# First layer's modulation in eight channel blocks, fed into two projections that grow together, with the softplus moved behind them

## The chip, the cores and the metric

The kernel runs on one core of one Trainium2 chip. TensorE (PE in the profile) does the matmuls and transposes, VectorE (DVE), ScalarE (ACT) and GpSimd (POOL) do elementwise work, and DMA queues started from SyncE (SP), ACT or POOL move data between HBM and on-chip memory. A time is the device time of one launch in microseconds (us). Three runs of the kernel before gave 1446.84, 1443.05 and 1445.64 us; their median is 1445.64 us.

## The reference, cut to what matters

Two layers of a backbone over 256 context tokens and 1024 latent tokens, 1024 channels wide. Each layer first makes a shift and a scale out of a conditioning vector and modulates its input with them:

```python
def adaln(cond, w, b):
    return jnp.split(jax.nn.silu(cond) @ w + b, 3, axis=-1)
...
shift, scale, gate = adaln(c, ada_w[layer], ada_b[layer])
shift_c, scale_c, gate_c = adaln(c_ctx, ada_w[layer], ada_b[layer])
u_lat = h_lat * (1.0 + scale[:, None, :]) + shift[:, None, :]
u_ctx = h_ctx * (1.0 + scale_c) + shift_c
```

The first layer projects u with one 1024 x 3072 matrix. Eight of the 24 column blocks go through a short convolution into a gated linear recurrence run in both directions, four into a Fourier mix, and twelve are SiLU gates. The recurrence needs, for each channel and direction, the constant softplus(-lambda):

```python
r = jax.nn.sigmoid(g[0])
i = jax.nn.sigmoid(g[1])
log_a = -LRU_C * r * jax.nn.softplus(-lam.astype(jnp.float32))
a = jnp.exp(log_a)
b = jnp.sqrt(-jnp.expm1(2.0 * log_a)) * (i * xc.astype(jnp.float32))
```

The second layer is latent attention. Nothing in it is changed.

## The kernel before, in words

Channels lie on partitions, so that u is eight tiles of 128 channels by 1280 tokens (kt = 0 to 7). Every fp32 operand of a projection is split in a high part (`uh`, `w0h`) and a low part (`ul`, `w0l`), and a product is three matmuls: high x high, high x low, low x high. A projection of one column block (`in0`, tile `z`) is eight steps kt of nine matmuls: three operand pairs by token pieces of 512, 512 and 256. PSUM holds two such `z` tiles and two small tiles of 512 columns (`gtile`); a third `z` can begin when whoever reads the first one is done with it.

The order of the work is set by a scheduler of the tile framework, which places the instructions of each engine by estimated times; each engine then runs its own list strictly in order. At the start of the kernel the program gives, in the order of the string `ORD`:

- the softplus constants `vpos` and `vneg` (L105 to L132), some thirty tiny DVE operations and one Exp on ACT;
- the conditioning vector, through SiLU, as `cond` (L146 to L152);
- the modulation in four parts of 256 channels (`ada_part`, L211): eight 256 KB tiles of weights, 32 small matmuls (two instructions each), a copy out of PSUM (`adarow`, L221), a transpose (`adatr`, L223), and additions into `mod` (L227, L230);
- `u0(kt)` (L234): load of the x tile, DVE multiplies and adds in place (`xt`, L241), ACT casts to `uh`, DVE subtracts to `ul` (the helper `split`, L80 to L82).

Then come `silu_gate(0)`, which projects block 12 and multiplies it with its own sigmoid (`sg`, L300 and L301), and `conv(0)`, which projects block 0 and convolves it (`xc`, L313 to L317). Both projections are issued beside the modulation; the entries of `IA` hold back two of their steps until given parts of the modulation are done. `conv(1)` projects block 1 (`z1` here), with the gates of head block 0 (`gps`) spread between its steps. The second layer's modulation weights (`adam`, L166, L179) are used up in eight steps beside these.

All loads of this stretch are issued by SP, in one list, with at most eight in flight.

Of the kernel before, what the change touches and what calls it, by code (L numbers as in the profile page):

```python
# [54 lines left out]
def _body(ctx, tc, ap, out, dbg=None):  # L55
# [49 lines left out]

    lam = vv("lam", 0, 16)
    vpos = const.tile([P, 16], F32, name="vpos")
    vneg = const.tile([P, 16], F32, name="vneg")  # L110
# [7 lines left out]
    V.tensor_scalar(out=t2, in0=t1, scalar1=2.0, scalar2=None, op0=ALU.add)
    V.reciprocal(out=t2, in_=t2)
    V.tensor_tensor(out=t1, in0=t1, in1=t2, op=ALU.mult)  # L120
    V.tensor_tensor(out=t2, in0=t1, in1=t1, op=ALU.mult)
    NS = 8
    V.tensor_scalar(out=vneg, in0=t2, scalar1=2.0 / (2 * NS + 1), scalar2=2.0 / (2 * NS - 1), op0=ALU.mult, op1=ALU.add)
    for k in range(NS - 2, -1, -1):
        V.tensor_tensor(out=vneg, in0=vneg, in1=t2, op=ALU.mult)
        V.tensor_scalar(out=vneg, in0=vneg, scalar1=2.0 / (2 * k + 1), scalar2=None, op0=ALU.add)
    V.tensor_tensor(out=vneg, in0=vneg, in1=t1, op=ALU.mult)
    V.tensor_scalar(out=t0, in0=t0, scalar1=0.0, scalar2=None, op0=ALU.max)
    V.tensor_tensor(out=vpos, in0=vneg, in1=t0, op=ALU.add)
    V.tensor_scalar(out=vneg, in0=vpos, scalar1=-8.0, scalar2=None, op0=ALU.mult)  # L130
    V.tensor_scalar(out=vpos, in0=vpos, scalar1=8.0, scalar2=None, op0=ALU.mult)
    sp_c()  # L132
# [74 lines left out]
    a0_p, a0_c = pool("adaw0", 8, side="right")  # L207

    ada_end = {}

    def ada_part(h):  # L211
        acc = gtile(f"ada0{h}")
        for kt in range(KT):
            w = a0_p.tile([P, 512], F32, tag="adaw", name=f"adaw0{h}{kt}")
            load(w, ap["ada_0"][h, kt])
            for j in range(4):
                mm = TE.matmul(acc[32 * j : 32 * j + 32, 0:P], cond[:, kt, :], w[:, P * j : P * j + P],
                               start=(kt == 0), stop=(kt == KT - 1), tile_position=(0, 32 * j))
            ada_end[h, kt] = mm.ins
        row = a0_p.tile([P, P], F32, tag="row", bufs=2, name=f"adarow0{h}")  # L220
        V.tensor_copy(out=row, in_=acc[:, 0:P])  # L221
        tr = gtile(f"adatr0{h}")
        TE.transpose(tr[:, 0:P], row, ident)  # L223

        bias = vv("adab0", 0, 16).rearrange("p (s h i) -> p s h i", s=2, i=2)
        for m in range(2):
            V.tensor_tensor(out=mod[:, 0, m, :].rearrange("p (s h i) -> p s h i", s=2, i=2)[:, :, h, :],  # L227
                            in0=tr[:, 0:P].rearrange("p (s i r) -> p s i r", s=2, r=32)[:, :, :, m],
                            in1=bias[:, :, h, :], op=ALU.add)
        V.tensor_scalar(out=mod[:, 0, :, 8 + 2 * h : 10 + 2 * h], in0=mod[:, 0, :, 8 + 2 * h : 10 + 2 * h],  # L230
                        scalar1=1.0, scalar2=None, op0=ALU.add)

    xt_p, xt_c = pool("xt", 3, side="right")

    def u0(kt):
        x = xt_p.tile([P, T], F32, tag="xt", name=f"xt{kt}")
        load(x, ap["x_cm"][:, kt, :])
        cuts = (0, NC, 512, T) if kt in CUT else (0, NC, T)
        for a, b in zip(cuts, cuts[1:]):
# [3 lines left out]
        cuts = (0, 512, T) if kt in CUT else (0, T)  # L243
        for a, b in zip(cuts, cuts[1:]):
# [14 lines left out]
    def in0(m, work=()):  # L259
        wh, wl = ws.pop(m) if m in ws else w0_load(m)  # L260
        z = z_ps.tile([P, 1536], F32, tag="z", name=f"z{m}")
        for kt in range(KT):

            with tc.issue_after(ada_end[IA[m, kt]]) if (m, kt) in IA else ExitStack():
                for wi, ui in ((wh, uh), (wh, ul), (wl, uh)):
                    for a, n in CH3:
                        TE.matmul(z[:, a : a + n], wi[:, kt, :], ui[kt][:, a : a + n],  # L267
# [1121 lines left out]
```

## Time and profile before

| | |
|---|---|
| median of three runs | 1445.64 us |
| the profiled execution's own time | 1445.85 us |
| its span in the trace | 1444.0 us |
| PE busy in the span | 1396.4 us (97%) |
| DVE, ACT, POOL busy | 911.3, 542.2, 678.7 us |
| mean granted TensorE clock | 0.992 |
| first matmul of a projection | at 16.84 us |
| first matmul of `z1` | at 63.47 us |

The span is 1.85 us shorter than the execution's time. Shares of the whole span are means over stages with very different limits; the change touches the first 65 us only, and is read there, from the timeline and from the chain of waits.

### The profile page before, as it was taken

To read this page: it belongs to the slowest core of one execution; us is meant where nothing else is said; L and a number is where in the kernel's file an instruction comes from. 1 tells how busy PE (TensorE), PEld (TensorE's weight loads), DVE (VectorE), ACT (ScalarE), POOL (GpSimd) and SP (SyncE) were. 2 spreads that over 40 slices of the span, in tenths; PEclk is the share of its full clock that TensorE was granted. 3 is DMA by queue.
4 is the path that set the end of the run, shared out by engine and by line. 5 is a ranking of instruction groups with operands and counts; after the bars stand their busy time and mean duration, and the time that the engine had idled before them with its cause. 6 is when DMAs were issued, how large, how long until landed. Compare 5 with 4: busy or idle time off the path is not lost.

```text
span 1444.0 us, 19804 instructions
## 1 busy us (share of the span) xinstructions
PE 1396.4 (97%) x7912; PEld 1019.3 (71%) x7912; DVE 911.3 (63%) x1454; ACT 542.2 (38%) x664; POOL 678.7 (47%) x314
## 2 busy tenths in 40 slices
PE   6998999999999999999999999999999999999997
PEld 3776777777888878887987765666565556554686
DVE  5659868665755443236844546658576757564798
ACT  2276666656112221103432143443434344445210
POOL 1124434444201233412232158767766876799643
PEclk9999999999999999999999999999999999999999
DMA  8713233233302474321043131111101010124432
GB/s 301 249 52 113 98 114 105 93 106 107 126 16 91 147 243 136 114 78 34 16 146 113 52 99 37 37 46 47 53 16 37 30 38 16 39 70 146 133 131 88
DMA packets 65869, 134.10 MB, mean 93 GB/s; under 512 B 5864, under 2 KB 31720, under 8 KB 63472
## 3 DMA queue, kind: packets, MB, share of 16 engines
q1 hardware_dynamic: 63328, 124.83, 27.0%
q0 software_dynamic: 2016, 7.60, 1.4%
q8 instruction: 62, 1.02, 0.3%
q10 hardware_dynamic: 432, 0.39, 0.1%
q14 instruction: 31, 0.25, 0.1%
HBM read 101.14 MB, written 24.66 MB: 87 GB/s over the span
## 4 chain that ended last, share of the span: by engine, by line
PE 74%; DVE 16%; DMA 3%; ACT 2%; issue 2%; POOL 1%; SPq 0%; DVEq 0%; POOLq 0%; ACTq 0%
PE s L1078 12%; PE z L267 11%; PE y L646 10%; PE po L1094 9%; PE mx L977 6%; PE yf L1212 5%; PE in1g L85 2%; PE in1g L87 2%; PE in1g L86 2%; DVE xc L317 2%; DVE gate L367 1%; DVE th L362 1%; DVE gate L378 1%; DVE m L979 1%; DMA woraw<-in_wo 1%
## 5 line engine op out<-in xcount | busy, mean ns | idle before, releaser
L1084 POOL TENSOR_TENSOR ra<-ra,p 128x1024 f32<-128x1024 f32 x112 | 269.8, 2409 | 99.3 <-ACT p L1080 95.3
L979 DVE TENSOR_REDUCE m<-mx 128x1 f32<-128x512 f32 (+1 forms) x384 | 209.4, 589 | 76.0 <-PE mx L977 75.1
L1080 ACT ACTIVATE p<-s 128x1024 f32<-128x1024 f32 x160 | 163.5, 1025 | 175.4 <-PE s L1078 171.9
L267 PE MATMUL z<-uh,w0h 128*128 128x512 f32 (+1 forms) x576 | 149.6, 366 | 4.4 <-ACT uh L76 4.4
L82 POOL TENSOR_TENSOR w0l<-w,w0h 128x1024 fp32r<-128x1024 f32 x24 | 64.0, 2666 | 184.7 <-DVE w0h L78 102.3
L267 PE MATMUL z<-ul,w0h 128*128 128x512 f32 (+1 forms) x576 | 147.7, 362 | 0.0
L267 PE MATMUL z<-uh,w0l 128*128 128x512 f32 (+1 forms) x576 | 147.5, 361 | 0.0
L267 PEld LDWEIGHTS z<-uh,w0h 128*128 128x128 f32 x576 | 98.2, 190 | 33.3 <-issue 11.5
L267 PEld LDWEIGHTS z<-ul,w0h 128*128 128x128 f32 x576 | 96.7, 190 | 18.7 <-issue 1.2
L267 PEld LDWEIGHTS z<-uh,w0l 128*128 128x128 f32 x576 | 96.3, 190 | 18.3 <-issue 2.0
L1078 PE MATMUL s<-R,KR 64*128 64x512 f32 (+1 forms) x640 | 104.9, 392 | 0.0
L345 ACT ACTIVATE gate<-gps,vec 128x512 f32<-128x512 f32 (+1 forms) x96 | 57.5, 616 | 103.3 <-PE gps L87 103.1
L977 PE MATMUL mx<-Kh,Qh 64*128 64x512 f32 (+1 forms) x384 | 86.4, 396 | 1.8 <-DVE m L979 1.5
L1094 PE MATMUL po<-p,v_even 128*64 128x512 f32 x320 | 77.5, 605 | 0.0
L1094 PE MATMUL po<-p,v_odd 128*64 128x512 f32 x320 | 77.5, 605 | 0.0
L977 PEld LDWEIGHTS mx<-Kh,Qh 64*128 64x128 f32 x384 | 43.0, 185 | 48.6 <-DVE m L979 26.8
L977 PE MATMUL mx<-KR,R 64*128 64x512 f32 (+1 forms) x384 | 77.1, 357 | 0.0
L381 POOL TENSOR_TENSOR gate<-gate,gate 128x1280 f32<-128x1280 f32 x8 | 23.9, 2990 | 112.3 <-DVE gate L378 97.1
L1078 PEld LDWEIGHTS s<-R,KR 64*128 64x128 f32 (+1 forms) x640 | 64.7, 184 | 12.3
L1078 PE MATMUL s<-Qh,Kh 64*128 64x512 f32 x320 | 70.6, 413 | 0.5 <-DVE sg L1024 0.5
L649 DVE TENSOR_TENSOR n<-gbc,y 128x1024 f32<-128x1024 f32 x10 | 12.2, 1222 | 87.3 <-PE y L646 87.3
L1078 PE MATMUL s<-Qh,Kl 64*128 64x512 f32 x320 | 67.3, 390 | 0.0
(358 smaller groups left out, 3091.2 us busy)
## 6 DMA issues: line engine op xcount, KB each, us to landing
w<-in_w SPq DMA_DIRECT2D x24, 512.0 KB
adaw<-in_ada SPq DMA_DIRECT2D x32, 256.0 KB
adawm<-in_ada SPq DMA_DIRECT2D x8, 1024.0 KB
adawg<-in_ada_g SPq DMA_DIRECT2D x8, 1024.0 KB
y_dr<-sg SPq DMA_DIRECT2D x10, 640.0 KB
woraw<-in_wo SPq DMA_DIRECT2D x12, 512.0 KB
xt<-in_x_cm SPq DMA_DIRECT2D x8, 640.0 KB
yra<-y_dr SPq DMA_DIRECT2D x10, 512.0 KB
```

The lines of the kernel that those rows point to most:

```text
L82: el.tensor_tensor(out=lo, in0=src, in1=f(hi), op=ALU.subtract)
L85: TE.matmul(o, lh, rh, start=start, stop=False)
L267: TE.matmul(z[:, a : a + n], wi[:, kt, :], ui[kt][:, a : a + n], start=(kt == 0 and ui is uh and wi is wh), stop=(kt == KT - 1 and wi is wl))
L345: S.activation(out=gt[d, g][:, a : a + n], in_=ps[:, :n], func=AF.Sigmoid, bias=vv("gateb", 4 * j + i))
L646: TE.matmul(ps[:, 512 * hf : 512 * hf + 512], a[k], b[k][:, 512 * hf : 512 * hf + 512], start=(k == 0 and a is yh and b is woh), stop=(k = ...
L977: TE.matmul(ps[a][:, :n], q[r, P * t : P * t + P], k[r, a0 : a0 + n], start=st, stop=not st)
L979: V.tensor_reduce(out=m3s[t][:, a, i : i + 1], in_=ps[a][:, :n], axis=AX.X, op=ALU.max)
L1078: TE.matmul(ps[:, a, :], k[r, ks], w[r, c], start=(j == 0), stop=(j == len(parts) - 1))
L1080: S.activation(out=es, in_=ps, func=AF.Exp, scale=SCALE)
L1084: G.tensor_tensor(out=ra, in0=st["e"][0] if kt == 1 else ra, in1=es, op=ALU.add)
L1094: TE.matmul(st["o"][64 * a : 64 * a + 64, :], quad[q][6][:, k, 128 * i + 64 * a : 128 * i + 64 * a + 64], st["e"][k][:, a, :], start=(k == ...
L1212: TE.matmul(ps[i], a[:, k, :], b[k][:, pieces[i]], start=(k == 0 and a is oh and b is w1o), stop=(k == 7 and a is ol))
```

## The change

- The weights of the first modulation are laid out for eight blocks of 128 channels instead of four parts of 256: four loads of 256 KB each a block (`ada_load`), 16 small matmuls (two instructions each) and a copy (`ada_block`), one transpose of 64 rows and two additions (`ada_turn`). The "1 +" of the scale is put into the bias once (`ab0`), instead of into each part of `mod`.
- Block kt of the modulation now serves exactly tile kt of u. For kt = 0 to 7 the projections 12 and 0 both take step kt, with the turn of block kt+1 in the middle of projection 12's step and the matmuls of block kt+2 behind it.
- All of this stands in `tc.manual_schedule`: PE, DVE, ACT and POOL keep the order of the program text there.
- The conditioning vector is loaded first; block 12's weights, the identity and the small vectors are loaded from ACT's queue, the rest from SP's.
- The softplus (`decay`) is called after the last step of the two projections. Its text and the scheduler's list both place it there.

```diff
+    first = ExitStack()
+    first.enter_context(tc.manual_schedule(engines={e.engine for e in (TE, V, S, G)}))
...
+    def decay():
...
+        S.activation(out=t1, in_=t1, func=AF.Exp)
+        V.tensor_scalar(out=t2, in0=t1, scalar1=2.0, scalar2=None, op0=ALU.add)
...
+        for k in range(NS - 2, -1, -1):
+            V.tensor_tensor(out=vneg, in0=vneg, in1=t2, op=ALU.mult)
+            V.tensor_scalar(out=vneg, in0=vneg, scalar1=2.0 / (2 * k + 1), scalar2=None, op0=ALU.add)
...
+    def ada_load(h):
+        a0s[h] = [a0_p.tile([P, 2, 256], F32, tag="adaw", name=f"adaw0{h}{i}") for i in range(4)]
+        for i in range(4):
+            load(a0s[h][i], ap["ada_0"][h][:, 2 * i : 2 * i + 2, :])
...
+    def ada_block(h):
+        acc = gtile(f"ada0{h}")
         for kt in range(KT):
-            w = a0_p.tile([P, 512], F32, tag="adaw", name=f"adaw0{h}{kt}")
-            load(w, ap["ada_0"][h, kt])
-            for j in range(4):
-                mm = TE.matmul(acc[32 * j : 32 * j + 32, 0:P], cond[:, kt, :], w[:, P * j : P * j + P],
-                               start=(kt == 0), stop=(kt == KT - 1), tile_position=(0, 32 * j))
+            for j in range(2):
+                TE.matmul(acc[32 * j : 32 * j + 32, 0:P], cond[:, kt, :], a0s[h][kt // 2][:, kt % 2, P * j : P * j + P],
+                          start=(kt == 0), stop=(kt == KT - 1), tile_position=(0, 32 * j))
+        a0r[h] = a0_p.tile([64, P], F32, tag="row", bufs=2, name=f"adarow0{h}")
+        V.tensor_copy(out=a0r[h], in_=acc[0:64, 0:P])
+
+    def ada_turn(h):
         tr = gtile(f"adatr0{h}")
+        TE.transpose(tr[:, 0:64], a0r[h], ident[0:64, 0:64])
...
     def in0(m, work=()):
-        wh, wl = ws.pop(m) if m in ws else w0_load(m)
+        if m in z0s:
+            for u in work:
+                u()
+            return z0s.pop(m)
+        wh, wl = w0_load(m)
...
+    ada_load(0)
+    u_load(0)
+    w = w_p.tile([P, KT, P], F32, tag="w", name="w0_12")
+    S.dma_start(out=w, in_=ap["w0"][12])
+    S.dma_start(out=ident, in_=ap["ident"])
+    S.dma_start(out=vec, in_=ap["vec"])
...
+    for m in (12, 0):
+        z0s[m] = z_ps.tile([P, 1536], F32, tag="z", name=f"z{m}")
...
+    for kt in range(1, KT):
+        if kt + 2 < KT:
+            ada_load(kt + 2)
+            u_load(kt + 2)
+        in0_part(12, kt, 0)
+        if kt + 1 < KT:
+            ada_turn(kt + 1)
+            u0(kt + 1)
+        in0_part(12, kt, 1)
+        if kt + 2 < KT:
+            ada_block(kt + 2)
+        in0_part(0, kt)
+    decay()
+    first.close()
```

`in0_part(12, kt, 0)` is the first five matmuls of a step (the three of `uh` x `w0h`, two of `ul` x `w0h`), `in0_part(12, kt, 1)` the other four.

How the list of VectorE changes where the two projections end. Before (`w0h_626` and `w0h_820` are the weights of blocks 1 and 2, `sg_522` the gate of block 12, `z_449` its projection, `ul_135` the last low part of u):

```order
L82 TENSOR_TENSOR ul_135<-xt_435,uh_127 128x1280 [waits Activation_49]
L78 CAST w0h_626<-w_1_624 128x1024 [waits DMAHW6_49,PE_49,Pool_49]
L301 TENSOR_TENSOR sg_522<-sg_522,z_449 128x1280 [waits Activation_49]
L78 CAST gh_616<-gw_614 128x512 [waits DMAHW0_49]
L78 CAST w0h_820<-w_2_818 128x1024 [waits DMAHW7_49,PE_49,Pool_49]
L179 COPY adarow_148<-adam_600 128x512 [waits PE_49]
L317 SCALAR_TENSOR_TENSOR xc_606<-z_525,vec,xc_606 128x255 [waits Activation_49]
```

And now, from the last low part of u (`ul_99`) to the first softplus steps behind block 2's weights (`w0h_848`; `w0h_654` are block 1's):

```order
L80 TENSOR_TENSOR ul_99<-xt_489,uh_91 128x1280 [waits Activation_49]
L118 TENSOR_SCALAR sp_583<-vec 128x16
L119 TENSOR_TENSOR sp_584<-vec,sp_583 128x16 [waits DVE_49]
L76 CAST w0h_654<-w_1_652 128x1024 [waits DMAHW6_49,PE_49,Pool_49]
L121 TENSOR_SCALAR sp_585<-sp_584 128x16 [waits Activation_49]
L122 RECIPROCAL sp_585<-sp_585 128x16 [waits DVE_49]
L123 TENSOR_TENSOR sp_584<-sp_584,sp_585 128x16 [waits DVE_49]
L76 CAST w0h_848<-w_2_846 128x1024 [waits DMAHW7_49,PE_49,Pool_49]
L124 TENSOR_TENSOR sp_585<-sp_584 128x16 [waits DVE_49]
```

Behind these come five more softplus steps, the copy of `adam` out of PSUM (L178) and fifteen softplus steps, of which the last stand here with what follows them (`sg_623` and `z_181` belong to block 12, `z_182` to block 0):

```order
L131 TENSOR_SCALAR sp_583<-sp_583 128x16
L132 TENSOR_TENSOR vpos<-vneg,sp_583 128x16 [waits DVE_49]
L133 TENSOR_SCALAR vneg<-vpos 128x16 [waits DVE_49]
L134 TENSOR_SCALAR vpos<-vpos 128x16 [waits DVE_49]
L355 TENSOR_TENSOR sg_623<-sg_623,z_181 128x1280 [waits Activation_49]
L371 SCALAR_TENSOR_TENSOR xc_634<-z_182,vec,xc_634 128x255 [waits Activation_49]
```

The gate of block 12 stood ahead of block 2's weights; it now stands behind them and behind the whole softplus.

How the list of TensorE changes. Before, where the second part of the modulation stands between matmuls of projection 12 (`ada_231` is the modulation, `z_449` the projection):

```order
L267 MATMUL z_449<-uh_120,w0h_209 128x256
L217 MATMUL ada_231<-adaw_232,cond 32x128 [waits DMAHW6_49,PE_49]
L217 MATMUL ada_231<-adaw_232,cond 32x128 x3
L267 MATMUL z_449<-ul_128,w0h_209 128x512 [waits DVE_49]
L217 MATMUL ada_231<-adaw_238,cond 32x128 [waits DMAHW7_49]
L217 MATMUL ada_231<-adaw_238,cond 32x128 x3
L267 MATMUL z_449<-ul_128,w0h_209 128x512 [waits DVE_49]
```

And now, in the middle of one step of the loop (`adatr_331` is the turn for the next block, `ada_343` the block after that, `z_181` projection 12):

```order
L318 MATMUL z_181<-ul_94,w0h_135 128x512 [waits DVE_49]
L318 MATMUL z_181<-ul_94,w0h_135 128x512
L227 MATMUL adatr_331<-ident,adarow_305 128x64 [waits DVE_49]
L318 MATMUL z_181<-ul_94,w0h_135 128x256
L318 MATMUL z_181<-uh_86,w0l_136 128x512 x2
L318 MATMUL z_181<-uh_86,w0l_136 128x256
L220 MATMUL ada_343<-adaw_316,cond 32x128 [waits DMAHW2_49,PE_49]
L220 MATMUL ada_343<-adaw_316,cond 32x128 x3
```

The modulation is no longer strewn between projection matmuls four at a time; the turn stands behind matmuls that need the present step's `ul`.

At the end of the stretch TensorE's list now reads (`z_182` is projection 0, `adam` a piece of the second layer's modulation, `z_658` block 1's projection):

```order
L318 MATMUL z_182<-ul_99,w0h_219 128x256
L318 MATMUL z_182<-uh_91,w0l_220 128x512 x2
L318 MATMUL z_182<-uh_91,w0l_220 128x256
L165 MATMUL adam_628<-adawm_626,cond 32x512 [waits DMAHW1_49,PE_49]
L165 MATMUL adam_628<-adawm_626,cond 32x512 x3
L273 MATMUL z_658<-uh_84,w0h_654 128x512 [waits DVE_49,PE_49]
```

`z_658` takes the PSUM place of `z_181`, and so its first matmul waits for the VectorE multiplication that reads `z_181` (`sg_623`).

## Rows read from the trace of the kernel before

**Rows 1.** The page's busy time of each engine (share of the span, instructions).
```profile
PE 1396.4 (97%) x7912; PEld 1019.3 (71%) x7912; DVE 911.3 (63%) x1454; ACT 542.2 (38%) x664; POOL 678.7 (47%) x314
```

**Rows 2.** Timeline, first modulation part: start, duration, engine, line, operation, idle before.
```profile
9.60 0.20 PEld L217 LDWEIGHTS ada<-adaw,cond 128*32 128x32 f32 x8 [0.45 <-DMA adaw<-in_ada]
...
10.95 0.20 PEld L217 LDWEIGHTS ada<-adaw,cond 128*32 128x32 f32 x8 [0.47 <-DMA adaw<-in_ada]
...
12.53 0.23 DVE L227 TENSOR_TENSOR mod<-adatr,vec 128x4 f32<-128x4 f32 x2 [0.56 <-PE adatr L223]
```

**Rows 3.** Timeline, the first u tile up to the first projection matmul.
```profile
13.33 2.34 POOL L82 TENSOR_TENSOR w0l<-w,w0h 128x1024 fp32r<-128x1024 f32 x1 [12.88 <-ACT w0h L76]
13.87 2.86 DVE L241 TENSOR_SCALAR xt<-xt,mod 128x256 f32<-128x256 f32 x3 [0.91 <-DMA xt<-in_x_cm]
...
16.84 1.81 PE L267 MATMUL z<-uh,w0h 128*128 128x512 f32 x3 [4.35 <-ACT uh L76]
```

**Rows 4.** Tile xt, 0 to 60 us: count, duration ns min/median/max.
```profile
L241 DVE TENSOR_SCALAR xt<-xt,mod x18: 401/542/1945, 13.9 to 51.3; 128x256 f32<-128x256 f32 x10, 128x1024 f32<-128x1024 f32 x6, 128x768 f32<-128x768 f32 x2
L76 ACT CAST uh<-xt x10: 619/1257/1267, 16.2 to 52.2; 128x1280 fp32r<-128x1280 f32 x6, 128x512 fp32r<-128x512 f32 x2, 128x768 fp32r<-128x768 f32 x2
```

**Rows 5.** Chain of waits, 26 to 63 us: start, time on the chain, what.
```profile
26.28 0.58 PE ada L217 x8
...
27.81 0.36 PE ada L217 x8
...
42.55 0.12 PE adatr L223
...
42.69 0.24 DVE mod L227 x2
...
42.96 0.18 DVE mod L230
...
43.16 1.15 DVE xt L241 x2
...
44.33 1.27 ACT uh L76
...
45.63 2.89 DVE ul L82 x2
...
49.11 13.44 PE z L267 x69
```

**Rows 6.** Windows: length, busy time of each engine, granted clock, DMA share, GB/s.
```profile
22.00:24.00 2.00, 2.00 (x12) 1.00 (x12) 0.00 (x0) 1.04 (x1) 0.81 (x1) 1.00 1.02 406
...
120.00:122.00 2.00, 2.00 (x7) 1.61 (x7) 2.00 (x3) 2.00 (x3) 1.46 (x1) 0.50 0.00 0
122.00:124.00 2.00, 2.00 (x10) 1.68 (x9) 2.00 (x1) 1.99 (x2) 2.00 (x2) 0.74 0.00 0
```

**Rows 7.** Timeline, the hand-over from the two projections to z1.
```profile
59.07 1.49 DVE L301 TENSOR_TENSOR sg<-sg,z 128x1280 f32<-128x1280 f32 x1 [1.11 <-ACT sg L300]
...
62.06 0.77 DVE L78 CAST w0h<-w 128x1024 fp32r<-128x1024 f32 x1 [1.16 <-issue]
...
62.48 1.06 PE L166 MATMUL adam<-adawm,cond 128*32 128x512 f32 x8
...
63.47 0.85 PE L267 MATMUL z<-uh,w0h 128*128 128x512 f32 x3
...
63.61 0.69 DVE L179 COPY adarow<-adam 128x512 f32<-128x512 f32 x1 [0.79 <-PE adam L166]
```

**Rows 8.** Groups by line, one of the softplus: busy us, mean ns, idle before.
```profile
L125 DVE TENSOR_TENSOR vneg<-vneg,sp 128x16 f32<-128x16 f32 x7 | 1.2, 174 | 0.2
```

**Rows 9.** Timeline, DVE and POOL, two stretches around 220 us.
```profile
220.41 3.43 POOL L82 TENSOR_TENSOR w0l<-w,w0h 128x1024 fp32r<-128x1024 f32 x1 [0.86 <-DVE w0h L78]
...
221.50 2.36 DVE L665 TENSOR_TENSOR f<-vec,mod 128x8 f32<-128x8 f32 x1
```

**Rows 10.** Timeline, PE after a long idle time.
```profile
117.24 0.79 PE L85 MATMUL gps<-xh,gh 128*128 128x512 f32 x1 [4.00 <-DVE adarow L181]
```

More of the change, by code (lines that the diff above doesn't have):

```diff
@@ L118, in _body @@
[L118 to L126, printed above, removed]
@@ L233, in _body, with u_load @@
-    xt_p, xt_c = pool("xt", 3, side="right")
+            V.tensor_tensor(out=mod[:, 0, m, :].rearrange("p (s k) -> p s k", s=2)[:, :, h],
+                            in0=tr[:, 0:64].rearrange("p (s r) -> p s r", r=32)[:, :, m],
+                            in1=ab0.rearrange("p (s k) -> p s k", s=2)[:, :, h], op=ALU.add)
+    xt_p, xt_c = pool("xt", 3, side="right")
+    xs0 = {}
+    def u_load(kt):
+        xs0[kt] = xt_p.tile([P, T], F32, tag="xt", name=f"xt{kt}")
+        for a, b in ((0, 512), (512, T)) if kt == 0 else ((0, T),):
+            load(xs0[kt][:, a:b], ap["x_cm"][:, kt, a:b])
@@ L235, in u0 @@
     def u0(kt):
[L236 to L239, printed above, removed]
+        x = xs0.pop(kt)
+        for a, b in ((0, NC), (NC, 512), (512, T)) if kt == 0 else ((0, NC), (NC, T)):
             m = 1 if b == NC else 0
@@ L272, in in0, with w0_load @@
         return z
[L274 to L276 removed]
+    def w0_load(m, eh=V, w=None):
+        if w is None:
+            w = w_p.tile([P, KT, P], F32, tag="w", name=f"w0_{m}")
+            load(w, ap["w0"][m])
         wh = w_p.tile([P, KT, P], F32R, tag="wh", name=f"w0h_{m}")
@@ L280, in w0_load, with in0_part @@
         return wh, wl
-    ws = {}
-    for c in ORD.split():
-        i = int(c[1])
-        if c[0] == "a":
-            ada_part(i)
-        elif c[0] == "w":
-            ws[12 - 12 * i] = w0_load(12 - 12 * i, S)
-        else:
-            u0(i)
+    z0s = {}
+    ada_load(0)
[4 more added lines that the diff above has]
+    S.dma_start(out=vec, in_=ap["vec"])
+    S.activation(out=sgc, in_=cnd, func=AF.Sigmoid)
+    V.tensor_tensor(out=cond[:, :, 0:2], in0=cnd, in1=sgc, op=ALU.mult)
+    ab0 = const.tile([P, 16], F32, name="ab0")
+    V.tensor_copy(out=ab0[:, 0:8], in_=vv("adab0", 0, 8))
+    V.tensor_scalar(out=ab0[:, 8:16], in0=vv("adab0", 8, 8), scalar1=1.0, scalar2=None, op0=ALU.add)
+    ws = {12: w0_load(12, S, w)}
+    ada_load(1)
+    w = w_p.tile([P, KT, P], F32, tag="w", name="w0_0")
+    load(w, ap["w0"][0])
+    u_load(1)
+    ada_block(0)
+    ada_turn(0)
+    u0(0)
+    for m in (12, 0):
+        z0s[m] = z_ps.tile([P, 1536], F32, tag="z", name=f"z{m}")
+    def in0_part(m, kt, part=None):
+        wh, wl = ws[m]
+        three = ((wh, uh), (wh, ul), (wl, uh))
+        steps = [(a, n, *o) for a, n in CH3 for o in three] if kt == 0 else [(a, n, *o) for o in three for a, n in CH3]
+        for a, n, wi, ui in steps if part is None else steps[5 * part : 5 + 4 * part]:
+            TE.matmul(z0s[m][:, a : a + n], wi[:, kt, :], ui[kt][:, a : a + n],
+                      start=(kt == 0 and ui is uh and wi is wh), stop=(kt == KT - 1 and wi is wl))
+    ada_load(2)
+    in0_part(12, 0)
+    ada_block(1)
+    ws[0] = w0_load(0, S, w)
+    u_load(2)
+    in0_part(0, 0, 0)
+    ada_turn(1)
+    u0(1)
+    in0_part(0, 0, 1)
+    ada_block(2)
+    for kt in range(1, KT):
[12 more added lines that the diff above has]
+    first.close()
     xt_c()
```

81 lines of the change are left out of this document (32 added, 49 removed).

## The prediction, made before the run

> **What bounds the kernel now.** I read the page first: TensorE is busy in 97% of the span [rows 1], so over the whole kernel only what makes TensorE start earlier, wait less or run at a higher clock can move the end. Then I read the timeline of the first 65 us, as the change touches nothing else, and the chain of waits there.
>
> The stretch has three parts. Up to 16.84 us TensorE waits for the first tile of u: the eighth 256 KB tile of modulation weights lets its matmuls begin at 10.95 us, `mod` is ready 1.81 us later [rows 2], and two multiplications on 256 columns, which take 0.40 us at best [rows 4], take until 16.2 us (the first matmul at 16.84 us [rows 3] less the cast of 0.62 us [rows 4]), because one of them lasts 1.95 us [rows 4]: GpSimd runs its weight subtraction from 13.33 to 15.67 us, and VectorE's `xt` begun at 13.87 us stands meanwhile [rows 3]. From 16.84 to 62.48 us TensorE works nearly without a gap. At first it runs at half its rate: eight modulation instructions take 0.58 us on the chain until 26.3 us and 0.36 us from 27.8 us on [rows 5]. The granted clock of the windows shows 1.00 in that time too [rows 6], so here I go by durations: the 1.2 GHz level for 10.9 us after the first projection matmul, then 2.4 GHz. The third part is the hand-over: `adam` at 62.48 us, the first matmul of `z1` at 63.47 us [rows 7]. VectorE had multiplied block 12's gate 3 us earlier, so `z1` waited for nothing.
>
> **The change part by part.** I follow the moment at which `z1` begins, since behind it the lists of all engines do the same work.
>
> *The start.* Before the first block is complete, four tiles of modulation weights, block 12's weights (as many bytes as two tiles) and the three small loads must arrive: what had arrived before when the sixth tile's matmuls began, 9.60 us [rows 2]. Plus 1.81 us, `mod` is ready at 11.4 us. x's first half is one tile more, some 0.7 us later than 9.6 us by the step between tiles, so it is no bound. Block 12's weights now come early, GpSimd's 2.34 us on them is over by then, and two multiplications of 0.40 us and a cast of 0.62 us [rows 4] give the first projection matmul at 12.9 us, 3.9 us earlier than now.
>
> The Trainium skill ("Trainium Kernel Development and Optimization", Key Constraints) says that loads started from several queues share the same DMA engines and that a second queue only saves time in issuing. The trace before has its engines at a share of 1.02 and 406 GB/s on one queue alone [rows 6], which bears that out for the steady part; by the rule the gain of the start lies in the fewer bytes.
>
> *Step 0 and the first turn.* A step's nine matmuls take 1.75 us at the full rate (69 in 13.44 us [rows 5]), 3.5 us at half: to 16.4 us. Block 1 of the modulation, four groups of eight at 0.58 us: 18.7 us. Projection 0's first five matmuls, 2560 of a step's 3840 columns, 2.3 us: turn 1 at 21.0 us. GpSimd's low part of block 0's weights is ready about then too (its bytes land near 15 us at 0.4 MB/us [rows 6], cast and subtraction follow), so it costs nothing.
>
> *The loop.* The turn of block kt+1 stands behind two matmuls that need `ul` of block kt, and `ul` of kt+1 comes out of that turn. This is a chain through four engines: turn 0.12 us, `mod` 0.24, `xt` 1.15, `uh` 1.27, `ul` 1.45 (half of 2.89) [rows 5], 0.47 for two matmuls, and seven hand-overs of 0.02 to 0.05 us: 5.0 us. The step of 0.18 us for "1 +" [rows 5] is gone. TensorE's own work in the same time is a step of each projection, 3.5 us, block and turn with 1.4 us: 4.9 us at the full rate. So the chain and TensorE need about the same, and I take 5.0 us a block. The loads need 1.7 MB a block, 4.2 us at 406 GB/s, and are hidden. At the half rate TensorE would need twice its 4.9 us; if the half rate lasts 10.9 us from the first projection matmul, as before, it ends at 23.8 us, and the second turn comes at 26.2 us. Five blocks later the seventh turn is at 51.2 us, its `ul` 4.35 us later at 55.55 us, and fifteen matmuls (2.9 us) end both projections at 58.5 us, 4.0 us earlier than now.
>
> *The hand-over.* This is what the change pays. Counted from the end E of projection 0: projection 12 now ends only 1.75 us earlier, and `z1` needs its PSUM place. The gate's multiplication that frees it stands on VectorE behind all of the softplus but two steps, behind the weights of block 2, which wait for projection 0's last use of `w0h`, and behind the copy of `adam`. Softplus steps cost 0.174 us and a gap of 0.03 us [rows 8], 0.205 us. With VectorE alone: weights of block 2 done at E+0.35, six steps to E+1.6, copy of `adam` 0.69 us [rows 7] to E+2.3, fifteen steps to E+5.4, the multiplication of 1.49 us [rows 7] to E+6.9.
>
> GpSimd comes on top. Its subtractions for blocks 1 and 2 take 2.34 us each [rows 3] and start as soon as the cast before them is done. A multiplication on 128x8 numbers took 2.36 us when it met one [rows 9], and the multiplication of the start 1.95 us [rows 4], against 0.17 us for a step alone [rows 8]. The first subtraction runs from about E-1.5 to E+0.85 and holds the third softplus product, so block 2's weights end at E+2.0; the second runs from E+2.1 to E+4.45 and holds the next step. Then five steps to E+5.5, the copy to E+6.2, fifteen steps to E+9.3, the multiplication to E+10.8. The bounds are E+6.9 (GpSimd never in the way) and E+11.6 (both subtractions in full); I take E+10.8, as the rows show waiting to the end of GpSimd's instruction.
>
> The Trainium skill ("SBUF — State Buffer", SBUF: two separate sides) says that VectorE and GpSimd share a port pair under an exclusive lock, and that an operation with two inputs in SBUF, or a copy in a fast mode, waits for GpSimd's whole instruction. By it `z1` begins at E+10.8; without it, at E+6.9.
>
> So `z1` begins at 58.5 + 10.8 = 69.3 us instead of 63.47 us: 5.8 us later. TensorE has only `adam` in that time and is idle from E+1.0 on, nearly 10 us.
>
> *The clock behind it.* After an idle time of 4.0 us TensorE resumed at 117.24 us [rows 10] and ran at a granted clock of 0.50, the 1.2 GHz level, until about 123.0 us (0.74 in the window from 122 us) [rows 6]: 5.8 us at half, 2.9 us lost. I take the same 2.9 us for `z1`. Bounds are 0 and the 5.5 us of the kernel's start (10.9 us at half). The gates in `z1` come after four steps, 9.9 us with that clock, and the convolution, cast and split that they need take some 9 us on VectorE from `z1`'s beginning, so they add nothing.
>
> *The rest.* One more ACT table load and the Exp stand beside TensorE's last two steps and end before VectorE's third softplus step. SP's list after the stretch is the same. Both cost nothing; if the Exp were late, its table load would add up to 1.3 us.
>
> The sum: 5.8 + 2.9 = 8.7 us on the profiled execution's own time of 1445.85 us, 1454.5 us. That execution lies 0.2 us from the median, so the same number stands for the median.
>
> **Rivals.**
>
> A. *The softplus stays off the path, as the change's words say.* `z1` would wait only for the sigmoid and multiplication of block 12, to E+1.1: 59.6 us, 3.9 us earlier, no idle time, 1442.0 us. For it: ACT and VectorE have free time in the loop. Against it: block 2's weights stand before 21 softplus steps in VectorE's list, and they cannot start before projection 0 has used its last `w0h`. It decides if the steps run before E+0.3.
>
> B. *GpSimd doesn't hold the small steps.* `z1` at E+6.9, 65.4 us, 3.9 us less than forecast: 1450.6 us, and 1447.7 us if the clock also stays up over the shorter idle time. For it: steps leave gaps of only 0.03 us in which GpSimd must get in. Against it: [rows 9].
>
> C. *The half rate lasts longer in the loop.* Every block at half costs TensorE 9.8 us instead of 5.0, 4.8 us more. In the first stretch modulation matmuls were mixed among those of the projection, and the clock came up only after 10.9 us; here they come in blocks of 1.0 to 2.3 us. One block more gives 1459.3 us, two 1464.1 us. Loads below 340 GB/s would look alike.
>
> **How the numbers follow.** I give the forecast 0.5, A 0.1, B 0.2, C 0.2. The forecast's own range is 1451 to 1458 us. The whole range leaves out A and the worse half of C: 1446 to 1461 us. A measurement of this kernel tells a change from none at about 0.3%, 4.3 us. Faster than 1441.3 us is only A with a still better start, 0.05. Within 0.3% lie the rest of A, half of B and little of the forecast, 0.2. Slower has the rest, 0.75.
>
> **What would show it.** In the profile after: the first projection matmul near 13 us; turns 5 us apart, with TensorE waiting for `ul` at most some tenths of a microsecond; projection 0 ending near 58.5 us; VectorE's softplus steps behind that, one or two of them lasting 2 us or more beside GpSimd; `z1` beginning near 69 us after 10 us of idle TensorE, released by the multiplication `sg`; a granted clock of 0.50 right behind. The forecast is wrong if `z1` begins before 65 us, or if projection 0 ends after 62 us.

## The result and the profile after

The changed kernel takes 1458.7 us (median of 4 runs, 1456.4 to 1461.2), the kernel before 1446.2 us: a ratio of 1.0091, 95% interval 1.0075 to 1.0108. It is slower, by 12.5 us, where 8.7 us were forecast; the time lies inside the range of 1446 to 1461 us. The profiled execution is the slowest of the four: own time 1461.15 us, span 1459.4 us, 15.4 us over the one before. TensorE's busy time has hardly changed [rows 1]; it waits longer:

```profile
PE 1398.7 (96%) x7916; PEld 1026.0 (70%) x7916; DVE 917.9 (63%) x1462; ACT 544.1 (37%) x664; POOL 680.2 (47%) x314
```

Next the chain of waits of the changed kernel from 7.6 us on (start, time on the chain, what), which answers to [rows 3, 5]:

```profile
7.60 2.80 PE ada L220 x24
...
12.20 0.63 ACT uh L74
12.82 0.04 issue
12.87 3.87 PE z L318 x9
16.74 2.94 PE ada L220 x32
...
26.38 0.20 PE adatr L227
26.58 0.89 PE z L318 x4
27.47 1.87 PE ada L220 x32
29.34 3.01 PE z L318 x14
32.35 0.20 PE adatr L227
32.55 0.89 PE z L318 x4
```

The first projection matmul comes at 12.87 us instead of 16.84 us. From 26 us on the chain holds nothing but TensorE: four matmuls, a modulation block, fourteen matmuls, a turn, and so on, 5.97 us from turn to turn up to the seventh at 56.18 us. VectorE and ScalarE stand on it only at the start, between the first and the second turn, and behind the seventh, which is the last. In this loop the modulation block takes 1.87 us for 32 instructions.

TensorE's timeline at the hand-over [rows 7] (start, duration, engine, line, operation, count, idle before):

```profile
63.89 1.07 PE L165 MATMUL adam<-adawm,cond 128*32 128x512 f32 x8
73.71 1.40 PE L273 MATMUL z<-uh,w0h 128*128 128x512 f32 x3 [8.75 <-DVE sg L355]
74.91 1.27 PE L273 MATMUL z<-ul,w0h 128*128 128x512 f32 x3
75.97 1.18 PE L273 MATMUL z<-uh,w0l 128*128 128x512 f32 x3
76.99 0.73 PE L273 MATMUL z<-uh,w0h 128*128 128x512 f32 x3
```

The two projections end at 63.89 us, 1.4 us later than before. Then TensorE is idle for 8.75 us until VectorE's gate multiplication `sg` frees the place of `z1`. Nine matmuls take 3.28 us instead of 1.75, and from 76.99 us on the rate is full. What VectorE did meanwhile, and GpSimd beside it:

```profile
61.70 0.69 DVE L76 CAST w0h<-w 128x1024 fp32r<-128x1024 f32 x1 [0.70 <-PE z L318]
...
62.80 2.15 DVE L123 TENSOR_TENSOR sp<-sp,sp 128x16 f32<-128x16 f32 x1
64.87 0.68 DVE L76 CAST w0h<-w 128x1024 fp32r<-128x1024 f32 x1
...
65.88 2.19 DVE L128 TENSOR_TENSOR vneg<-vneg,sp 128x16 f32<-128x16 f32 x1
...
72.08 1.48 DVE L355 TENSOR_TENSOR sg<-sg,z 128x1280 f32<-128x1280 f32 x1
```
```profile
62.53 2.39 POOL L80 TENSOR_TENSOR w0l<-w,w0h 128x1024 fp32r<-128x1024 f32 x1 [42.43 <-DVE sp L121]
65.69 2.35 POOL L80 TENSOR_TENSOR w0l<-w,w0h 128x1024 fp32r<-128x1024 f32 x1 [0.77 <-PE adam L165]
```

Two products on 128x16 numbers last over 2 us, each until a subtraction of GpSimd ends; the same kind of step takes 0.17 us alone. The windows behind show the clock (length, busy time of each engine, granted clock, DMA share, GB/s):

```profile
70.00:74.00 4.00, 0.29 (x1) 0.33 (x2) 3.66 (x14) 0.00 (x0) 0.00 (x0) 0.51 0.69 257
74.00:78.00 4.00, 4.00 (x14) 3.28 (x14) 4.00 (x5) 0.00 (x0) 0.00 (x0) 0.64 0.03 11
78.00:82.00 4.00, 4.00 (x22) 3.39 (x21) 3.84 (x4) 0.00 (x0) 1.81 (x1) 1.00 0.10 17
```

So `z1` begins 10.2 us later and loses 1.5 us to the half rate: 11.7 us. At the last gate product of this layer (at 362.35 us before, 373.15 us after) the shift is 10.8 us, so nothing is added between `z1` and there, and about 1 us is won back. What the profiled execution loses beyond that arises in stages that hold the same work in the same order; other runs of the same kernel are up to 4.7 us faster, and I do not assign it.

### The profile page after: what moved, and what is told of

Read it like the earlier page. It is cut to its first block, busy times and chain, and to the rows that moved or that the text cites. A ratio compares the mean times of both kernels' runs of the same rounds, so it can differ in the third digit from the quotient of the medians.

```text
span 1459.4 us, 19829 instructions
## 1 busy us (share of the span) xinstructions
PE 1398.7 (96%) x7916; PEld 1026.0 (70%) x7916; DVE 917.9 (63%) x1462; ACT 544.1 (37%) x664; POOL 680.2 (47%) x314
## 4 chain that ended last, share of the span: by engine, by line
PE 70%; DVE 19%; issue 4%; DMA 3%; ACT 3%; POOL 1%; SPq 0%; DVEq 0%; POOLq 0%; ACTq 0%
PE s L1132 12%; PE y L700 10%; PE z L273 10%; PE po L1148 9%; PE mx L1031 6%; PE in1g L83 2%; PE in1g L85 2%; PE in1g L84 2%; PE z L318 2%; DVE xc L371 2%; DVE hf L1316 2%; DVE gate L421 1%; DVE gate L432 1%; DVE m L1033 1%; PE ada L220 1%
## 5 line engine op out<-in xcount | busy, mean ns | idle before, releaser
L80 POOL TENSOR_TENSOR w0l<-w,w0h 128x1024 fp32r<-128x1024 f32 x24 | 63.9, 2663 | 189.5 <-DVE w0h L76 102.7
L273 PE MATMUL z<-uh,w0h 128*128 128x512 f32 x528 | 136.3, 366 | 8.8 <-DVE sg L355 8.8
L273 PE MATMUL z<-uh,w0l 128*128 128x512 f32 x528 | 134.1, 360 | 0.0
L273 PE MATMUL z<-ul,w0h 128*128 128x512 f32 x528 | 133.7, 360 | 0.0
L273 PEld LDWEIGHTS z<-uh,w0h 128*128 128x128 f32 x528 | 90.3, 190 | 35.0 <-issue 20.2
L273 PEld LDWEIGHTS z<-uh,w0l 128*128 128x128 f32 x528 | 88.5, 190 | 16.2 <-issue 0.8
L273 PEld LDWEIGHTS z<-ul,w0h 128*128 128x128 f32 x528 | 88.7, 190 | 15.6
L1132 PE MATMUL s<-Ql,Kh 64*128 64x512 f32 x320 | 67.1, 391 | 0.0
```

Of the source, the lines that this page charges most:

```text
L80: el.tensor_tensor(out=lo, in0=src, in1=f(hi), op=ALU.subtract)
L1132: TE.matmul(ps[:, a, :], k[r, ks], w[r, c], start=(j == 0), stop=(j == len(parts) - 1))
```

## The experiments

Times in us; E is the start of `adam`, that is the end of the first two projections. The table puts all runs together, the text tells what each was for.

| kernel | first projection matmul | E | z1 begins | time | ratio to before (95%) |
|---|---|---|---|---|---|
| before | 16.84 | 62.48 | 63.47 | 1446.2 | 1 |
| changed | 12.87 | 63.89 | 73.71 | 1458.7 | 1.0091 (1.0075 to 1.0108) |
| e1 softplus in the loop | 12.50 | 63.26 | 66.71 | 1450.5 | 1.0028 (1.0017 to 1.0039) |
| e2 softplus at the start | 18.22 | 68.93 | 72.41 | 1454.6 | 1.0060 (1.0045 to 1.0075) |
| e3 four strips | 12.70 | 60.29 | 70.12 | 1455.5 | 1.0068 (1.0053 to 1.0083) |
| e4 two sums | 12.88 | 63.26 | 73.09 | 1458.1 | 1.0084 (1.0066 to 1.0101) |
| e5 low part on VectorE | 12.79 | 63.85 | 73.14 | 1457.8 | 1.0088 (1.0072 to 1.0104) |
| e12 both low parts | 13.11 | 63.33 | 71.53 | 1455.8, one run | |
| e7 one queue | 16.01 | 66.36 | 76.20 | 1463.0, one run | |
| e8 (as e1) | 13.80 | 64.70 | 68.16 | 1449.9 | 1.0036 (1.0024 to 1.0049) |
| e10 e1, gate first | 12.99 | 64.06 | 65.23 | 1448.5 | 1.0022 (1.0011 to 1.0033) |
| e13 gate, then softplus | 13.02 | 64.08 | 65.25 | 1450.7 | 1.0030 (1.0020 to 1.0041) |
| e9 all but the gate's place | 12.14 | 58.55 | 62.02 | 1443.6 | 0.9990 (0.9981 to 1.0000) |
| e11 all | 12.34 | 54.85 | 57.63 | 1439.7 | 0.9957 (0.9944 to 0.9970) |

**e1, the softplus in the loop.** `decay()` becomes a list of steps `dk`, and a fifth of it is issued in each of five loop steps:

```
+        for u in spread(dk, 5, kt - 1) if kt <= 5 else ():
+            u()
         in0_part(0, kt)
-    decay()
```

> The changed kernel with the softplus's instructions taken apart and put five or six at a time behind the modulation copies of loop steps 1 to 5, where VectorE is idle for 1.56 us a step. Theory: block 1's projection waited 9.9 us after the first two had ended because the gate multiplication stood behind the softplus, two of whose steps GpSimd held for 2 us each. Then the first two projections still end near 63.9 us, block 1 starts at 65 to 66 us instead of 73.7, TensorE's clock stays at 1.00 there, and the time is 1448 us (10 us less than 1458.7). Rival: the weight casts of blocks 1 and 2 and GpSimd's low parts hold that multiplication by themselves: block 1 starts at 70 us or later, 1455 us.

`z1` begins 3.45 us behind E instead of 9.8 us, and the time falls by 8.2 us: the theory holds in the main, but 66.71 us is 0.7 to 1.7 us later than it said. VectorE's timeline shows what is left:

```profile
62.84 2.00 DVE L76 CAST w0h<-w 128x1024 fp32r<-128x1024 f32 x1 [1.07 <-PE z L328]
64.76 0.41 DVE L76 CAST gh<-gw 128x512 fp32r<-128x512 f32 x1
65.09 1.47 DVE L368 TENSOR_TENSOR sg<-sg,z 128x1280 f32<-128x1280 f32 x1
```

Block 2's weight cast stands ahead of the multiplication, and beside GpSimd (subtracting from 61.90 to 64.29 us) it takes 2.00 us instead of 0.69. So the rival has a share of about 2 us. In another point the theory failed: TensorE was idle for only 2.39 us, and yet its clock fell to the half rate behind that in this execution, as the window from 68 us on shows (granted clock third from the end):

```profile
68.00:70.00 2.00, 2.00 (x7) 1.69 (x6) 2.00 (x3) 0.00 (x0) 0.63 (x1) 0.50 0.86 323
```

**e8 and e10, the gate ahead of that cast.** In e8 only the end of the fixed order moved behind `sg0`; the instruction lists came out as in e1, so e8 is a second measurement of e1. In its profiled execution TensorE was idle for 2.40 us at the same place, and the granted clock stayed at 1.00. e10 writes the casts into the fixed order:

```
+    ws[1] = w0_load(1)
     sg0 = silu_gate(0, lru)
+    ws[2] = w0_load(2)
+    first.close()
```

> The kernel with the softplus in the loop, and in addition the gate multiplication of block 12 ahead of the weight casts of blocks 1 and 2 in VectorE's list (there block 1 still waited 2.4 us, as that cast of block 2 took 2.00 us beside GpSimd). Theory: sigmoid from 61.6 us, 1.24 us, multiplication 1.48 us: block 1 starts at 64.5 instead of 66.7 us, behind the modulation of the other layer and without an idle time, the clock stays up, and the time is 1447 us (3.5 us less). Rival: GpSimd's subtraction from 61.9 to 64.3 us holds the multiplication as well: 66.5 us and 1450.5 us.

> The kernel with the softplus in the loop, and block 2's weight cast written behind the gate multiplication of block 12 in the part whose order is fixed, so that it stands behind it in VectorE's list (the edit tried before left the list as it was). Theory: sigmoid 61.6 to 62.9 us, multiplication 1.48 us: block 1 starts at 64.4 instead of 66.7 us, with no idle TensorE, time 1448 us. Rival: GpSimd's subtraction for block 1 (61.9 to 64.3 us) holds the multiplication as it held the cast: block 1 at 66 us or later, 1450 us.

In e10 TensorE no longer waits: `z1` follows `adam` at 65.23 us, 0.8 us behind the theory's 64.4 because E itself is 0.8 us later there, and the time is 1448.5 us where 1448 us were said. VectorE's row of the multiplication:

```profile
63.69 1.49 DVE L367 TENSOR_TENSOR sg<-sg,z 128x1280 f32<-128x1280 f32 x1 [0.77 <-ACT sg L366]
```

GpSimd subtracted from 62.71 to 65.17 us, and this multiplication, which reads `z` from PSUM, took its usual time. The rival falls. `z1` still begins 1.8 us later than in the kernel before: that is the slower loop, to which e3 turns.

**e13, the softplus behind, but after the gate.** The changed kernel with the casts and the gate as in e10, and `decay()` behind them:

> The changed kernel with the softplus still behind the two projections, but behind the gate multiplication of block 12 in VectorE's list, mixed with the convolution that follows. Theory: what cost 10 us is the place in the list, not the softplus: block 1 starts near 65.2 us, as in the kernel with the softplus in the loop and the gate multiplication first (1448.5 us); the convolution's cast and split end some 2 us later by nine small steps and up to 4 us more where GpSimd holds a product, so that the gates inside block 1 wait 1 to 5 us: 1449.5 to 1453.5 us. Rival: the wait only changes its place, from the start of block 1 to its gates: 1457 us.

`z1` at 65.25 us as said, 1450.7 us. What the softplus still costs appears inside `z1`, in TensorE's timeline:

```profile
74.72 0.73 PE L83 MATMUL gps<-xh,gh 128*128 128x512 f32 x2 [0.76 <-DVE xh L76]
...
77.31 0.50 PE L84 MATMUL gps<-xl,gh 128*128 128x512 f32 x1 [0.69 <-DVE xl L80]
```

Two waits of 0.7 us instead of one of 8.75. The median lies 2.3 us above that of e10, the intervals of the two overlap, and the two waits make 1.45 us: so about 1.5 to 2.3 us is what the softplus itself costs here. The rest was its place in one engine's list.

**e2, the softplus at the start.** `decay()` stands behind the two bias copies.

> The changed kernel with the softplus at the program's start again, behind the two bias copies on VectorE. Theory: its 27 steps of about 0.2 us hold the first modulation copy from 10.4 to about 14.2 us, so the first projection matmul comes at 16.7 us instead of 12.9; the loop is as long as before, the hand-over to block 1 loses its 9 us, and the time is 1452 us. So putting the softplus behind cost more (9 us) than it gave at the start (4 us). Rival: the start is covered by the loads and GpSimd's hold does not matter: 1448 us.

The size was off. The first projection matmul comes 5.35 us later, not 3.8, since here too a product met GpSimd, as VectorE's timeline shows:

```profile
10.01 2.23 DVE L128 TENSOR_TENSOR vneg<-vneg,sp 128x16 f32<-128x16 f32 x1
...
15.78 0.28 DVE L223 COPY adarow<-ada 64x128 f32<-64x128 f32 x1
```

Even so the kernel is 4.1 us faster than the changed one: moving the softplus behind saved 5.35 us at the start and cost 6.3 us between E and `z1` (9.8 against 3.5 us). `z1` begins 1.3 us earlier in e2 and at the full rate, which saves another 1.5 us; the rest of the 4.1 us I do not assign.

That saving at the start is one against e2, not against the kernel before. There the softplus stood at the start too and held nothing, as VectorE's timeline of the kernel before shows:

```profile
3.60 0.18 DVE L115 TENSOR_SCALAR sp<-vec 128x16 f32<-128x16 f32 x1 [2.45 <-DMA vec<-in_vec]
...
8.94 0.18 DVE L131 TENSOR_SCALAR vpos<-vpos 128x16 f32<-128x16 f32 x1
11.67 0.29 DVE L221 COPY adarow<-ada 128x128 f32<-128x128 f32 x1 [2.56 <-PE ada L217]
```

Its input, the bias table `vec`, was there at 3.60 us, and VectorE was idle for 2.56 us between the last step and the first modulation copy. The changed kernel loads the table later (it is there at 7.89 us, in e2 at 8.07 us); the same steps, one of them held by GpSimd, end at 15.86 us in e2, and so they stand in the way.

**e5 and e12, GpSimd out of the way.** The softplus stays; low parts of weights are subtracted on VectorE, in e5 for blocks 1 and 13 (block 2, which was meant, was missed), in e12 for 1 and 2:

```
-        wh, wl = w0_load(m)
+        wh, wl = w0_load(m, el=V if m in (1, 2) else G)
```

> The changed kernel with the low parts of the weights of blocks 1 and 2 subtracted on VectorE instead of GpSimd, the softplus where it is. Theory: two softplus products took 2.15 and 2.19 us because GpSimd's subtractions held them; without these they take 0.17 us (4.0 us less), and the two subtractions cost VectorE about 1.2 us each (1.49 us for 1280 numbers). So block 1 starts 8.3 instead of 9.9 us after the first two projections end, at about 72 us, and the time is 1457 us. Rival: the long steps have another reason than GpSimd: they stay near 2 us, the subtractions come on top, block 1 starts near 76 us, 1461 us.

> The changed kernel with the low parts of the weights of blocks 1 and 2 both on VectorE (the edit before had reached block 1's, not block 2's: one of the two long softplus products, 2.31 us, had stayed beside GpSimd's remaining subtraction, and block 1 started 9.3 us after the two projections' end). Theory: no softplus product lasts over 0.3 us; the second subtraction costs VectorE 1.23 us and saves 2.1 us: block 1 starts 8.3 to 8.5 us behind the end, near 72.3 us. Rival: a long product stays although GpSimd is idle: 9.3 us or more.

In e5 `z1` begins between what the theory and the rival said, as one subtraction stayed on GpSimd: one long product was left, the one beside the one subtraction left; in e12 none. The two timelines of VectorE, e5 and then e12:

```profile
64.57 2.31 DVE L123 TENSOR_TENSOR sp<-sp,sp 128x16 f32<-128x16 f32 x1
```
```profile
63.96 1.22 DVE L80 TENSOR_TENSOR w0l<-w,w0h 128x1024 fp32r<-128x1024 f32 x1
65.10 0.17 DVE L123 TENSOR_TENSOR sp<-sp,sp 128x16 f32<-128x16 f32 x1
```

`z1` begins 9.3 and 8.2 us behind E, 9.8 in the changed kernel. e5's time is not clear of the changed kernel's, and e12 is a single run, so the argument rests on these rows. GpSimd's holds are the cause of the long steps, and with e1 the two parts of the wait are told apart.

**e3 and e4, why a modulation block takes 1.87 us.** Each block multiplies into two of TensorE's four 32-column strips; the kernel before used four. e3 sends odd contraction blocks to the other two strips and adds the halves at the turn; e4 keeps two strips, but alternates between two sums:

```
-                TE.matmul(acc[32 * j : 32 * j + 32, 0:P], ..., tile_position=(0, 32 * j))
+                c = 32 * (j + 2 * (kt % 2))
+                TE.matmul(acc[c : c + 32, 0:P], ..., tile_position=(0, c))
```

> The changed kernel with each modulation block's products spread over four 32-column strips of TensorE again (even and odd channel blocks of the contraction apart, the halves added by two more small VectorE steps at each turn). The 32 instructions of a block took 1.87 us in two strips, and 64 in four strips took 1.96 us in the kernel before. Theory: matmuls of different strips run beside each other, and two strips halve this: the block goes to about 1.0 us, the loop's period from 5.97 to about 5.1 us, the first two projections end at 58.5 instead of 63.9 us, and block 1 still waits 10 us: 1453.5 us. Rivals: what counts is that the stationary operand changes every two matmuls (it does so here too), or the chain over VectorE and ScalarE sets the period: 5.9 us and 1459 us.

> The changed kernel with two strips as it has, but each strip's products go in turn to two accumulators (even and odd contraction blocks, in two PSUM tiles), added by one more VectorE step behind the copy. If the strips set the price of a modulation block, it stays at 1.87 us, the period at 5.97 us and the time at 1459 us. Rival: successive matmuls wait for the sum that the one before them writes in the same accumulator: then the block falls to about 1.0 us as with four strips, and the time to 1453.5 us.

TensorE's timeline in e3, then in e4, then in the kernel before (64 instructions in four strips):

```profile
47.05 0.27 PE L228 MATMUL adatr<-ident,adarow 128*128 128x128 f32 x1
...
47.96 1.08 PE L221 MATMUL ada<-adaw,cond 128*32 128x128 f32 x32
...
51.83 0.73 PE L323 MATMUL z<-ul,w0h 128*128 128x512 f32 x2 [0.25 <-DVE ul L80]
52.40 0.27 PE L228 MATMUL adatr<-ident,adarow 128*128 128x128 f32 x1
```
```profile
50.68 1.94 PE L220 MATMUL ada07e<-adaw,cond 128*32 128x128 f32 x32
```
```profile
45.05 1.96 PE L217 MATMUL ada<-adaw,cond 128*32 128x128 f32 x64
```

With four strips the same 32 instructions take 1.08 us in this view, with two 1.94 us, one sum or two. So the strips set the price. The period falls to 5.35 us, not 5.1, because now the chain binds and TensorE waits 0.25 us a turn for `ul`: E is 60.29 us and not 58.5, the time 1455.5 and not 1453.5 us.

**e7, the loads on one queue.**

```
-    S.dma_start(out=w, in_=ap["w0"][12])
+    load(w, ap["w0"][12])
```

(and likewise the identity and the bias table)

> The changed kernel with the loads of block 12's weights, the identity and the bias table started by SyncE, as all others, instead of ScalarE. Theory: only the time of issuing is lost; SyncE gets to these three after six other loads, near 5.5 us, so the weights land near 8.5 instead of 4.8 us and GpSimd's subtraction moves to about 9.5 to 12 us, where it meets VectorE's bias copies and the first multiplications: first projection matmul 0.5 to 1.5 us later than 12.9 us, all behind it as before. Rival: the second queue brought a higher load rate: then the modulation weights too land later, and the first projection matmul comes 3 us later or more.

This is a single run. The delay is 3.1 us, as the rival had it, but not for its reason: the first modulation weights came earlier than in the changed kernel (first matmuls on them at 4.64 instead of 6.48 us). Block 12's weights, issued at 4.02 us, were there only at 11.37 us (4.81 us on ScalarE's queue), and the bias table at 11.78 instead of 7.89 us, behind the loads ahead of them. ScalarE's row, VectorE's and TensorE's:

```profile
11.37 1.04 ACT L74 CAST w0h<-w 128x1024 fp32r<-128x1024 f32 x1 [8.71 <-DMA w<-in_w]
```
```profile
11.93 0.28 DVE L223 COPY adarow<-ada 64x128 f32<-64x128 f32 x1
...
12.93 2.97 DVE L246 TENSOR_SCALAR xt<-xt,mod 128x256 f32<-128x256 f32 x3
```
```profile
16.01 0.80 PE L318 MATMUL z<-uh,w0h 128*128 128x512 f32 x1 [3.38 <-ACT uh L74]
```

The late table holds VectorE's list, so that the first modulation copy comes at 11.93 instead of 10.42 us: 1.5 us. The late weights bring GpSimd's subtraction to 12.50 to 14.84 us, beside the first multiplications, as the theory said: these take 2.97 instead of 1.32 us, and that is the other 1.65 us.

**e9 and e11, put together.** e9 joins e1, four strips with the sums of both halves done in two VectorE steps a turn, the first turn ahead of block 0's matmuls, and e8's edit, which again did not move the gate. e11 has e10's edit in its place, and cuts each of x's blocks in two:

```
-        for a, b in ((0, 512), (512, T)) if kt == 0 else ((0, T),):
+        for a, b in ((0, 512), (512, T)):
```

(and the multiplications likewise)

> The changed kernel with what the runs before point to: the softplus in the loop's gaps, the modulation in four strips (sums of the halves in one VectorE step a turn more than the changed kernel's one... two steps in all, as it has), the gate multiplication ahead of the weight casts, and the first turn ahead of block 0's first matmuls, so that these no longer wait for GpSimd's low part of the weights. Theory: with four strips the two projections ended at 60.3 us with 6.4 us of idle TensorE; the first turn comes 2 us earlier and the chain a block falls from 5.35 to about 5.15 us: they end at 57 us, block 1 starts at 58 us instead of 63.5 us in the kernel before, the clock stays up: 1440.5 us. Rival: the chain over VectorE and ScalarE stays at 5.35 us and the loads of the third block come too late for an earlier turn: 60 us, block 1 at 61.3 us, 1444 us.

> Softplus in the loop, four strips, the first turn ahead of block 0's matmuls, block 2's weight cast behind the gate multiplication, and each of x's blocks multiplied, cast and split in two pieces of 512 and 768 numbers a partition, as the first is, so that ScalarE works beside VectorE. Theory: in the kernel with the first three of these the turns are 5.4 us apart with 0.3 to 0.5 us of TensorE waiting for ul; the pieces shorten that chain by about 1 us, TensorE's own work of 5.1 us a block sets the period, the two projections end near 55.5 instead of 58.5 us, block 1 starts at 57 us (63.5 in the kernel before), time 1438.5 us. Rival: the smaller pieces cost VectorE and ScalarE as much as they overlap, and loads set the pace: 58.5 us, block 1 at 59.7 us, 1441.5 us.

e9's time came out between its theory and its rival, near the rival: the turns stay 5.4 us apart, and 2.40 us of waiting for the gate are left. e11 came out near its theory; TensorE is the bound there, without a wait in the loop:

```profile
43.19 0.27 PE L238 MATMUL adatr<-ident,adarow 128*128 128x128 f32 x1
...
48.02 0.27 PE L238 MATMUL adatr<-ident,adarow 128*128 128x128 f32 x1
...
54.85 1.07 PE L175 MATMUL adam<-adawm,cond 128*32 128x512 f32 x8
57.63 0.85 PE L285 MATMUL z<-uh,w0h 128*128 128x512 f32 x3 [1.72 <-DVE sg L369]
```
```profile
54.62 1.56 DVE L76 CAST gh<-gw 128x512 fp32r<-128x512 f32 x1 [1.25 <-DMA gw<-in_gw]
```

The period is 4.83 us and `z1` begins 5.8 us earlier than in the kernel before. e11 is faster than both kernels, by 0.43% and 1.3%. Its remaining 1.72 us go back to the cast ahead of the gate, in the last row: it waits 1.25 us for its load and then, beside GpSimd's subtraction (53.50 to 55.89 us), takes 1.56 us instead of 0.42.

## Why the prediction was right in the hand-over and wrong in the loop

- **The start**: 12.87 us, said 12.9. The number was right, the reason only half. I put the earlier modulation on fewer bytes and the rest on GpSimd being done in time. e7 has the same bytes on one queue and loses both: the first modulation copy comes at 11.93 us, no earlier than in the kernel before (11.67 us), GpSimd is in the way again, and the first projection matmul comes at 16.01 us. Of the 4.0 us gained, 3.1 hang on the second queue. Nor was a load the last bound in the changed kernel, as the sum had it, but TensorE's 24 instructions from 7.60 to 10.40 us. That 12.9 came out is in part luck. The Trainium skill ("Trainium Kernel Development and Optimization", Key Constraints) says that a second queue only saves time in issuing. The trace does not agree for the start: in e7 the issue of block 12's weights ended 3.3 us later than in the changed kernel (4.45 against 1.15 us), but they were there 6.6 us later (11.37 against 4.81 us). For the other 3.3 us they stood, as the order of arrival suggests, behind the earlier loads of the same queue.
- **Step 0 and the first turn**: 21.06 us, said 21.0, by errors that cancel, which is luck. Step 0 took 3.87 us instead of 3.5 and the block 2.94 us instead of 2.3, but the five matmuls behind them 1.46 us instead of 2.3, as the full rate came before them and not at 23.8 us. A block takes 3.89 us at the half rate (the first) and 1.94 us at the full rate in TensorE's timeline, this one 3.01 us from 16.67 us on; that puts the change at about 18.8 us. The second turn came at 26.31 us, said 26.2.
- **The loop is the step that failed.** "TensorE's own work in the same time is ... block and turn with 1.4 us: 4.9 us." Block and turn took 2.07 us, so TensorE needs 0.89 + 3.01 + 2.07 = 5.97 us, and the chain of 5.0 us lies under it. I had priced the 32 instructions by rows in which four strips were in use [rows 5]; e3 and e4 show that this was it. (The sum also left out the turn: four groups at 0.36 us and a turn of 0.12 us make 1.56 us.) The chain itself was sized well: 5.25 us from the first turn to the second, and 5.35 us with e3's two more additions. Five periods cost 4.9 us more than said, E was 63.9 us instead of 58.5, and by the sign that the prediction set itself (projection 0 ending after 62 us) its forecast was wrong, although the time lies in the range.
- **The hand-over**: E+9.8, said E+10.8, by the mechanism named: two holds by GpSimd, the softplus, then `sg`. e1, e12 and e13 each take one part away and find its price. This step, which is not luck, made the kernel slower: 8.8 us more than the 1.0 us of before, over twice the gain at the start.
- **The clock behind it**: 1.5 us lost in the profiled execution, said 2.9. Behind the same idle time (8.77 and 8.78 us) e4 lost 2.1 us (fifteen matmuls in 5.0 us) and e7 2.9 us (eighteen in 6.4 us), so 2.9 us was no wrong size; the loss differs from execution to execution.
- **The rest**: gates in `z1` did not wait, as said.
- **The sum**: `z1` 4.4 us later than said (5.4 us for the loop, 1.0 us back in the hand-over) and 1.4 us less for the clock make 3.0 us; of the 3.8 us between 12.5 and 8.7 us, 0.8 us are left that no step accounts for. 1458.7 us lies just above the forecast's own range (1451 to 1458 us), and inside the whole one because that reached up to 1461 us for rival C, whose cause did not occur. That is luck.
- **The rivals**: A is out: `z1` waited for the softplus, and without it in the way began 1.2 us behind E (e10). B is out: two steps lasted over 2 us beside GpSimd, and none once GpSimd did not subtract there (e12). C had the place right, a slower loop, and the cause wrong: fourteen matmuls take 3.01 us there, 0.215 us each, against 0.36 us at the half rate (nine in 3.28 us, at the beginning of `z1`); the blocks are slow by their strips.

## What to carry to other kernels

Work that looks free because an engine is idle costs what stands behind it in that engine's list: ask which instruction frees the buffer that the bound engine wants next, and put it first. When a change alters how many strips of TensorE a small matmul uses, price it again; a duration from another layout does not carry over. Nor is a step still free where it once was, when its input comes later (e2). And look for the next wait behind the one removed: without the softplus a cast held the gate (e1), and with four strips the chain held TensorE (e3).

## What the runs showed of the hardware beyond that

- 32 small fp32 matmuls took 1.94 us in two 32-column strips and 1.08 us in four (e4, e3); 64 in four took 1.96 us in the kernel before. The Trainium skill ("TensorE: Matmul & The Clock Gate", Part 3: Packing small matmuls — row/col tiling) says that matmuls at different tile positions run concurrently in the same array. The trace agrees; the prediction had not weighed it.
- While GpSimd subtracted, products of two SBUF operands (2.15, 2.19, 2.23, 2.31 us for 0.17), an SBUF cast (2.00 for 0.69, e1) and the first multiplications of x by its modulation (three in 2.97 for 1.32, e7) waited for it; a multiplication with an operand in PSUM did not (1.49 us, e10).
- After 8.75 us of idle TensorE the half rate lasted 3.3 us in the changed kernel, and after 8.77 and 8.78 us about 4.5 us in e4 and 6.2 us in e7; after 4.00 us, in the kernel before, 5.8 us [rows 6, 10]. After 2.4 us it lasted 3.4 us in e1 and did not come in e8. So the length of the idle time did not tell the price. A window of e7, 3.8 us behind the first matmul of its `z1`, shows a granted clock of 0.50:

```profile
80.00:82.00 2.00, 2.00 (x7) 1.71 (x6) 1.97 (x4) 0.00 (x0) 0.79 (x1) 0.50 0.00 0
```
